# Two-layer backbone step: layer 1's seven products in another order with another plan of weights, and low parts of eight weights by an adding DMA

## The chip, the cores and the metric

The kernel runs on one core of a Trainium2 chip, as one launch. The metric is the device time of that core in microseconds (us), the median of several executions. A core has five engines with a queue of instructions each: TensorE (PE in the profile, with its weight loads as PEld), VectorE (DVE), ScalarE (ACT), GpSimd (POOL) and SyncE (SP), which here only issues DMAs. PSUM is the memory with eight banks into which PE writes, SBUF the memory that the engines compute from. The granted clock is the share of its full speed that TensorE is allowed; the profile gives it by slices.

## The reference

One inference step of a small network with two layers, on 640 tokens of width 1024: 512 latent tokens (`x_sample`) and 128 context tokens (`x_prompt`). Layer 0 mixes by attention and spatial gating, layer 1 by pooling over windows. Each layer ends in an MLP with a hidden width of 4096.

```python
def pool_mixer(h, w_pool, scale):          # layer 1: window means minus the token, times w_pool
...
def squared_relu_mlp(h, w1, w2):
    a = jax.nn.relu(h @ w1)
    return (a * a) @ w2
...
        x = x + g1 * mix
        h = rms_norm(x, norm2_g[l]) * (1 + sc2) + sh2
        x = x + g2 * squared_relu_mlp(h, w_ff1[l], w_ff2[l])
    return rms_norm(x, final_g), ckv_list, kpe_list
```

All of it is in fp32.

## The kernel before

**Numbers in two parts.** PE multiplies in a rounded fp32 format (fp32r). To stay near fp32 accuracy every operand is held as a high part, its rounded copy, and a low part, the rest. Each product is three matmuls, hi·hi, hi·lo and lo·hi, by `mm3` (L801 to L803). Activations lie with features on the partitions and tokens along the row, in two halves of 320 tokens (`C1`, index `ci`), so most matmuls are 128x128 weights by 320 columns.

**Weights.** A queue in program order, the class `Weights`, brings every weight from HBM. `loads` (L182) issues DMAs on SP into five raw buffers (`RAWB`). `pump` takes the next item of the queue, if its raw data are loading and a slot for the result is free: ACT copies it to the high part (L214), and a subtraction makes the low part (L216) on the engine that `st.lo` names, VectorE as a rule. A pump that finds no free slot does nothing. `need` pumps until a weight is there, `free` gives its slot back. In an MLP there are eight slots of 128x2x1024; where the program calls `pump` is thus a plan of when the splits stand in ACT's and DVE's queues.

**The passage between the layers.** In layer 0's last block `tick0` sets `st.lo = nc.gpsimd`, and the pooling stage follows: `pool_mm` does, for eight tiles of 128 features, two matmuls with `w_pool`, a residual on DVE, a square on ACT and an addition of the squares on DVE (L692 and L707), and pumps a weight at every second tile. The sum of squares goes through PE, whose `R_ps` matmuls (L718) spread it over the partitions, and `norm_h` makes layer 1's h in halves: ht on DVE (L744), its high part on ACT (L748), its low part on DVE (L752). Next to these, `turn1` steps through the string list `TURNS`: at each `w` it pumps a weight with `st.lo = nc.gpsimd`. So eight weights in all, `w1` of layer 1's blocks 0 and 1, have their low parts made by GpSimd (L216).

**Layer 1's MLP.** Its 4096 hidden features are eight blocks of four 128-row groups. Blocks 0 and 1 (`lead`) are computed in the plain way while h is still being made. For the blocks b = 2 to 7, `blocks7` calls `up7(b, p)` for p = 0 and 1. One call makes two groups, f = 2p and g = 2p+1, for both halves of the tokens, as a 2x2 product of blocks by seven multiplications in place of eight (the form of Strassen and Winograd). Its left factors are sums of w1's four quarters, made by `w1s_use` in place in two raw buffers that are kept for it: item i splits one quarter or sum into hi (L558) and lo (L559) and then prepares the next sum (L563). Each result is half a slot (`half`). Its right factors are quarters of h and the sums `B[0..3]`, made once by `sums`. `product(i, op, ps, first)` is 4 times three matmuls; with `first` false it adds into a bank that holds an earlier product. Four banks are used: pa, pd, pb and pc, out of a pool of six (`psm`). Before the change, p1 is the copy of product 0 (ACT, L1598), u2 = p1 + product 2, u3 = u2 + product 1 (DVE, L1581), and the outputs are, in this order,

- (g,1) = u3 + product 3
- (f,0) = product 0 + product 4, added up in bank pa
- (g,0) = u2 + (product 1 + product 5, in bank pd)
- (f,1) = u2 + (product 3 + product 6, in bank pc)

`finish` makes of an output r the squared relu and its two parts in `A`: Relu, Square and a copy on ACT (L1586 to L1588), and a subtraction on DVE (L1589), which `up7` places after the next output's addition. Behind the two calls, `down` multiplies by w2 (16 sums of 12 matmuls for a block; L1407 adds each to x on DVE). The first four, the early ones (`cut`), start on groups 0 and 1 alone, then groups 3 and 2 follow.

**Order.** Every engine takes its instructions in the program's order, so the position of a `st.pump()` or of a `lo()` in `up7` decides what stands ahead of what on ACT and DVE. A block of layer 1 has 18 items: 14 of `w1s`, of which those of p = 0 and 1 hold seven half slots each, and four of w2 with a slot each. In blocks 0 and 1 two of the eight slots are lent to `sums` (`spare`), which leaves six.

## Time and profile before

| | us |
|---|---|
| median of three runs | 1301.89 |
| lowest, highest | 1299.29, 1303.52 |
| the profiled execution's own time | 1302.88 |
| its span, first to last instruction | 1301.1 |
| TensorE busy in that span | 1261.8 (97%) |
| VectorE, ScalarE, GpSimd busy | 826.6, 549.3, 216.5 |
| mean granted clock | 0.989 |

The profile is one execution. Its slices are 1/40 of the span, 32.5 us each, and a digit is the busy share in tenths. A stretch in the table of windows gives its limits and length, then for each engine the busy time and the number of instructions, then the granted clock, the share of DMA and its rate. In the timeline a row is an instruction: start, duration, engine, line and tile, with the idle time before it and what ended it in brackets. The passage between the layers lies at 804 to 870 us, the blocks b = 2 to 7 behind 885.

### The profile page before, as it was taken

To read this page: it belongs to the slowest core of one execution; us is meant where nothing else is said; L and a number is where in the kernel's file an instruction comes from. 1 tells how busy PE (TensorE), PEld (TensorE's weight loads), DVE (VectorE), ACT (ScalarE), POOL (GpSimd) and SP (SyncE) were. 2 spreads that over 40 slices of the span, in tenths; PEclk is the share of its full clock that TensorE was granted. 3 is DMA by queue.
4 is the path that set the end of the run, shared out by engine and by line. 5 is a ranking of instruction groups with operands and counts; after the bars stand their busy time and mean duration, and the time that the engine had idled before them with its cause. 6 is when DMAs were issued, how large, how long until landed. Compare 5 with 4: busy or idle time off the path is not lost.

```text
span 1301.1 us, 20746 instructions
## 1 busy us (share of the span) xinstructions
PE 1261.8 (97%) x8308; PEld 1183.4 (91%) x8308; DVE 826.6 (64%) x1553; ACT 549.3 (42%) x993; POOL 216.5 (17%) x182
## 2 busy tenths in 40 slices
PE   7999999999999999999999999799999999999997
PEld 5899975689999999999999998789999999999997
DVE  5753864564766575666666638876887567675664
ACT  4445454453453434333343414534235435354353
POOL 0010312221113221313131315610000000000001
PEclk8999999999999999999999999899999999999999
DMA  7742286340335344444353431202113223132102
GB/s 291 261 164 72 81 227 234 131 170 25 116 117 160 113 145 131 150 126 157 119 161 114 147 130 33 97 1 79 52 35 112 80 67 98 38 111 84 61 33 82
DMA packets 63200, 149.89 MB, mean 115 GB/s; under 512 B 5072, under 2 KB 21968, under 8 KB 62592
## 3 DMA queue, kind: packets, MB, share of 16 engines
q1 hardware_dynamic: 61360, 142.53, 33.3%
q0 software_dynamic: 1456, 5.96, 1.9%
q8 instruction: 65, 1.06, 0.3%
q14 instruction: 31, 0.25, 0.1%
q10 hardware_dynamic: 288, 0.08, 0.0%
HBM read 140.02 MB, written 5.39 MB: 112 GB/s over the span
## 4 chain that ended last, share of the span: by engine, by line
PE 79%; DVE 10%; ACT 7%; issue 2%; DMA 1%; POOL 0%; DVEq 0%; ACTq 0%; POOLq 0%
PE dn_ps L802 11%; PE dn_ps L801 11%; PE dn_ps L803 11%; PE up_ps L801 7%; PE up_ps L803 7%; PE up_ps L802 7%; PE wo_ps L801 1%; PE o_ps L1302 1%; PE wo_ps L803 1%; PE wo_ps L802 1%; ACT r L1587 1%; DVE w L216 1%; ACT w L558 1%; ACT r L1586 1%; PE t_ps L1269 1%
## 5 line engine op out<-in xcount | busy, mean ns | idle before, releaser
L801 PE MATMUL dn_ps<-aa,w 128*128 128x320 f32 (+4 forms) x1024 | 319.1, 312 | 2.1 <-ACT aa L1588 2.1
L802 PE MATMUL dn_ps<-aa,w 128*128 128x320 f32 (+4 forms) x1024 | 318.4, 311 | 0.7
L803 PE MATMUL dn_ps<-aa,w 128*128 128x320 f32 (+4 forms) x1024 | 316.8, 309 | 0.0
L802 PE MATMUL up_ps<-h,w 128*128 128x320 f32 (+2 forms) x800 | 248.6, 311 | 6.0 <-DVE h L752 5.9
L801 PE MATMUL up_ps<-h,w 128*128 128x320 f32 (+2 forms) x800 | 249.6, 312 | 1.3 <-ACT h L748 1.3
L803 PE MATMUL up_ps<-h,w 128*128 128x320 f32 (+2 forms) x800 | 248.6, 311 | 0.0
L1407 DVE SCALAR_TENSOR_TENSOR x<-dn_ps,mod,x 128x320 f32<-128x320 f32 (+4 forms) x360 | 144.7, 434 | 115.0 <-PE dn_ps L803 113.2
L801 PEld LDWEIGHTS dn_ps<-aa,w 128*128 128x128 f32 x1024 | 193.1, 189 | 5.8 <-ACT aa L1588 4.1
L216 DVE TENSOR_TENSOR w<-raw,w 128x1024 fp32r<-128x1024 f32 (+4 forms) x122 | 151.3, 1250 | 70.9 <-ACT w L214 69.8
L802 PEld LDWEIGHTS dn_ps<-aa,w 128*128 128x128 f32 x1024 | 193.0, 188 | 2.5 <-DVE aa L1589 2.4
L803 PEld LDWEIGHTS dn_ps<-aa,w 128*128 128x128 f32 x1024 | 193.0, 189 | 0.0
L214 ACT ACTIVATE w<-raw 128x1024 fp32r<-128x1024 f32 (+4 forms) x131 | 132.0, 1026 | 112.0 <-DMA raw<-w_ff 85.0
L802 PEld LDWEIGHTS up_ps<-h,w 128*128 128x128 f32 x800 | 151.2, 189 | 8.1 <-DVE h L752 8.1
L801 PEld LDWEIGHTS up_ps<-h,w 128*128 128x128 f32 x800 | 151.0, 189 | 4.9 <-issue 3.4
L466 POOL TENSOR_TENSOR acc<-acc,raw 128x1024 f32<-128x1024 f32 x42 | 100.7, 2399 | 303.7 <-ACT raw L464 297.6
L803 PEld LDWEIGHTS up_ps<-h,w 128*128 128x128 f32 x800 | 151.0, 189 | 0.0
L559 DVE TENSOR_TENSOR w<-raw,w 128x512 fp32r<-128x512 f32 x84 | 57.7, 687 | 34.6 <-ACT w L558 33.7
L558 ACT ACTIVATE w<-raw 128x512 fp32r<-128x512 f32 x84 | 51.4, 624 | 61.9 <-DVE raw L563 57.1
L464 ACT ACTIVATE raw<-raw,cs 128x1024 f32<-128x1024 f32 x42 | 48.3, 1149 | 62.6 <-DVE acc L459 54.2
L1925 POOL TENSOR_TENSOR y<-y,fg 128x1024 f32<-128x1024 f32 x1 | 2.4, 2392 | 416.5 <-ACT y L1921 416.5
L1481 DVE TENSOR_TENSOR r<-r,up_ps 128x328 f32<-128x328 f32 (+2 forms) x80 | 37.6, 484 | 42.6 <-ACT r L1480 41.0
L1484 DVE TENSOR_TENSOR aa<-r,aa 128x640 fp32r<-128x640 f32 (+3 forms) x52 | 39.6, 762 | 35.6 <-ACT aa L1483 35.6
(404 smaller groups left out, 2122.1 us busy)
## 6 DMA issues: line engine op xcount, KB each, us to landing
raw<-w_ff SPq DMA_DIRECT2D x126, 512.0 KB, 3.6
raw<-w_mod SPq DMA_DIRECT2D x80, 512.0 KB, 3.9
raw<-w_m SPq DMA_DIRECT2D x16, 512.0 KB, 6.0
raw<-w_out SPq DMA_DIRECT2D x8, 512.0 KB, 4.4
kT<-ckvT POOLq DMA_DIRECT2D x4, 768.0 KB, 10.8
xr<-x SPq DMA_DIRECT2D x5, 512.0 KB, 5.5
xs<-x SPq DMA_DIRECT2D x2, 1280.0 KB, 9.3
x<-xs POOLq DMA_DIRECT2D x2, 1280.0 KB, 9.6
```

The lines of the kernel that those rows point to most:

```text
L214: self.nc.scalar.activation(out=w[:, 0, 0:size], in_=r, func=AF.Copy)
L216: lo.tensor_tensor(out=w[:, 1, 0:size], in0=r, in1=w[:, 0, 0:size].bitcast(F32), op=ALU.subtract)
L464: act(out=raw if k else acc[1], in_=raw, func=AF.Copy, scale=w[1])
L466: nc.gpsimd.tensor_tensor(out=acc[1], in0=acc[1], in1=raw, op=ALU.add)
L558: act(out=w[:, 0], in_=src, func=AF.Copy)
L559: vec.tensor_tensor(out=w[:, 1], in0=src, in1=w[:, 0].bitcast(F32), op=ALU.subtract)
L801: mm(ps, lhsT=st_[0], rhs=mv[0], start=first, stop=False, skip_group_check=on)
L802: mm(ps, lhsT=st_[0], rhs=mv[1], start=False, stop=False, skip_group_check=on)
L803: mm(ps, lhsT=st_[1], rhs=mv[0], start=False, stop=last, skip_group_check=on)
L1407: vec.scalar_tensor_tensor(out=xv, in0=ps[:, p0:p0 + c1 - c0], scalar=gate[:, d, m:m + 1], in1=xv, op0=ALU.mult, op1=ALU.add)
L1481: vec.tensor_tensor(out=rv, in0=rv, in1=ps, op=ALU.mult)
L1484: vec.tensor_tensor(out=aa[:, 1, lo:hi], in0=r[:, lo:hi], in1=aa[:, 0, lo:hi].bitcast(F32), op=ALU.subtract)
```

## The change

There are four parts.

1. `st.lo` is None in the pooling stage and at the `w` of `TURNS`. `pump` then has ACT write the low part's place with the high part times -1, and GpSimd issues a DMA that reads the weight from HBM once more and adds it to that place (512 KB each). The subtraction on GpSimd is gone.
2. `up7` takes the last three products in another order: product 4 goes into bank pd, for (g,0); product 5 into pc, for (f,1); product 6 into pa, for (f,0). `w1s_use` makes the sums in the order that this asks for. The second operation of `finish` for (f,0) is a multiplication on DVE in place of a Square on ACT, and the low part of (f,1) follows behind product 6.
3. The plan of weights: product i's half slot is given back one product later (the last at the end of `up7`). Of the pumps in `up7`, one behind product 1 is gone, and the others stand at other products. In the downs a pump stands behind every sum from the third on, and two follow at the end of the block.
4. The early downs take the second half of the tokens first (`C[::-1]`).

```diff
@@ Weights.pump
-                self.nc.scalar.activation(out=w[:, 0, 0:size], in_=r, func=AF.Copy)
-                lo = self.nc.gpsimd if key[0] in self.slow else self.lo
-                lo.tensor_tensor(
-                    out=w[:, 1, 0:size], in0=r, in1=w[:, 0, 0:size].bitcast(F32), op=ALU.subtract
-                )
+                hi, lo = w[:, 0, 0:size], w[:, 1, 0:size]
+                self.nc.scalar.activation(out=hi, in_=r, func=AF.Copy)
+                eng = self.nc.gpsimd if key[0] in self.slow else self.lo
+                if eng is None:
+                    self.nc.scalar.activation(out=lo, in_=hi.bitcast(F32), func=AF.Copy, scale=-1.0)
+                    src, shape = loads[0]
+                    if len(shape) == 2:
+                        lo = lo.rearrange("p (k n) -> p k n", k=shape[0])
+                    self.nc.gpsimd.dma_start(out=lo, in_=src, accum_op=ALU.add)
+                else:
+                    eng.tensor_tensor(out=lo, in0=r, in1=hi.bitcast(F32), op=ALU.subtract)
@@ w1s_use
-            src = (f0, g0, g0, f0, f1, g1, f1)[i]
+            src = (f0, g0, g0, f0, g1, g0, f1)[i]
...
-                    4: (f1, f1, g0, ALU.subtract)}.get(i)
+                    4: (g0, f1, g0, ALU.subtract)}.get(i)
@@ up7, product
-                st.free(("w1s", l, b, p, i))
+                gone.append(("w1s", l, b, p, i))
+                if i:
+                    st.free(gone.pop(0))
@@ up7, finish
-                act(out=r, in_=r if src is None else src, func=AF.Relu)
-                act(out=r, in_=r, func=AF.Square)
+                if src is not None:
+                    act(out=r, in_=src, func=AF.Relu)
+                    vec.tensor_tensor(out=r, in0=r, in1=src, op=ALU.mult)
+                else:
+                    act(out=r, in_=r, func=AF.Relu)
+                    act(out=r, in_=r, func=AF.Square)
@@ up7
             pd = product(1, 2, None, True)
-            st.pump()
             pb = product(2, 1, None, True)
...
             lo = finish(g, 1)
             st.pump()
-            pa = product(4, (0, 1), pa, False)
-            lo()
-            lo = finish(f, 0, pa)
-            if not p:
-                st.pump()
-            pd = product(5, 3, pd, False)
+            pd = product(4, 3, pd, False)
             add(out(g, 0), u2, pd)
             lo()
             lo = finish(g, 0)
-            pc = product(6, (1, 1), pc, False)
+            if not p:
+                st.pump()
+            pc = product(5, (1, 1), pc, False)
             add(out(f, 1), u2, pc)
             lo()
             lo = finish(f, 1)
-            lo()
             if not p:
                 st.pump()
+            pa = product(6, (0, 1), pa, False)
+            lo()
+            finish(f, 0, pa)()
+            st.free(gone.pop(0))
@@ blocks7
-                    early = cut(range(2), C) if b >= f0 else []
+                    early = cut(range(2), C[::-1]) if b >= f0 else []
...
-                        if j % 2 or j > 3:
+                        if j > 1:
                             st.pump()
                     free(1)
                     if b == f0 - 1:
                         bg.drain()
+                    st.pump(2)
                     continue
@@ tick0
-        st.lo = nc.gpsimd
+        st.lo = None
@@ turn1
-                st.lo = nc.gpsimd if t == "w" else vec
+                st.lo = None if t == "w" else vec
```

## The prediction

> **What bounds the kernel now.** I read the page first, then the busy time by stretches, then the timelines of GpSimd (POOL), VectorE (DVE) and ScalarE (ACT) in the two places that the change touches, then the chain of waits and the waits of TensorE (PE).

> ```profile
> span 1301.1 us, 20746 instructions
> PE 1261.8 (97%) x8308; PEld 1183.4 (91%) x8308; DVE 826.6 (64%) x1553; ACT 549.3 (42%) x993; POOL 216.5 (17%) x182
> PE   7999999999999999999999999799999999999997
> ```

> PE sets the time: 97% busy, and only slice 26 (813 to 846 us, the passage between the layers) drops inside the run. So an edit gains where PE waits, and loses where it makes PE wait. The stretches, with PE's, PEld's, DVE's, ACT's and POOL's busy time in that order, show how much there is:

> ```profile
> 804.00:814.00 10.00, 6.70 (x31) 5.01 (x29) 9.69 (x12) 6.00 (x10) 6.91 (x3) 1.00 0.35 105
> 814.00:822.00 8.00, 7.21 (x33) 7.21 (x33) 2.98 (x11) 1.13 (x3) 4.71 (x15) 0.57 0.43 131
> 822.00:844.00 22.00, 16.37 (x102) 14.32 (x101) 21.36 (x31) 14.77 (x29) 16.39 (x8) 1.00 0.28 96
> 844.00:870.00 26.00, 25.70 (x139) 22.95 (x139) 18.67 (x46) 9.56 (x22) 3.54 (x5) 0.93 0.00 1
> 885.00:960.00 75.00, 75.00 (x513) 75.00 (x512) 56.39 (x119) 25.43 (x47) 0.00 (x0) 1.00 0.21 68
> ```

> Between 804 and 844 PE is idle for 3.3 + 0.8 + 5.6 = 9.7 us of 40, DVE is full, and the granted clock falls to 0.57 for one stretch. From 885 to 960 PE has no gap: 75.00 us for 513 matmuls, 0.146 us each. That is the pace against which I measure the blocks later on.

> **The passage: what GpSimd costs there.** In the timelines (start, duration, then engine and line):

> ```profile
> 804.69 4.95 POOL L216 TENSOR_TENSOR w<-raw,w 128x1024 fp32r<-128x1024 f32 x2 [1.48 <-ACT w L214]
> 812.04 4.90 POOL L216 TENSOR_TENSOR w<-raw,w 128x1024 fp32r<-128x1024 f32 x2 [2.40 <-ACT w L214]
> 825.88 7.58 POOL L216 TENSOR_TENSOR w<-raw,w 128x1024 fp32r<-128x1024 f32 x3 [7.16 <-ACT w L214]
> 805.17 2.23 DVE L707 TENSOR_TENSOR sq<-sq 128x320 f32<-128x320 f32 x1
> 807.79 2.20 DVE L707 TENSOR_TENSOR sq<-sq 128x320 f32<-128x320 f32 x1
> 810.38 0.48 DVE L707 TENSOR_TENSOR sq<-sq 128x320 f32<-128x320 f32 x1
> 812.36 2.38 DVE L707 TENSOR_TENSOR sq<-sq 128x320 f32<-128x320 f32 x1 [0.18 <-ACT sq L692]
> 823.06 0.55 DVE L752 SCALAR_TENSOR_TENSOR h<-ht,mod,h 128x320 fp32r<-128x320 f32 x1 [0.23 <-ACT h L748]
> 826.02 2.61 DVE L752 SCALAR_TENSOR_TENSOR h<-ht,mod,h 128x320 fp32r<-128x320 f32 x1
> 803.57 1.04 ACT L214 ACTIVATE w<-raw 128x1024 fp32r<-128x1024 f32 x1
> 814.79 2.49 PE R_ps L718 x12
> 869.34 1.23 PE R_ps L718 x12
> 839.67 0.55 ACT L748 ACTIVATE h<-ht,mod 128x320 fp32r<-128x320 f32 x1
> 843.71 0.54 DVE L752 SCALAR_TENSOR_TENSOR h<-ht,mod,h 128x320 fp32r<-128x320 f32 x1
> ```

> The same DVE addition takes 0.48 us alone and 2.2 to 2.4 us when GpSimd is in one of its 2.45 us subtractions; the h of L752 goes from 0.55 to 2.61. The change takes all eight subtractions away (2 + 2 + 3 and one at 834). It adds for each weight a second ACT pass of 1.04 us, right behind the first in ACT's queue, and one DMA issue on GpSimd.

> First half. DVE loses 1.75 + 1.72 + 1.90 = 5.4 us of stretching. But the pooling stage's squares (0.40 us each in ACT's queue) stand behind those passes: from 803.57 ACT now has three weights at 2.02 and six squares at 0.40 ahead of the last addition, which ends at 803.57 + 6.06 + 2.40 + 0.3 = 812.3. The R_ps matmuls of 814.79 so start 2.5 us earlier, not 5.4. Second half, from the first ht (L744) at 821.8 to the last h at 843.71: DVE is freed of about 6.5 us, but ACT's work before the last L748 (13.1 us, from the first at 822.5 to 840.2 with its waits) grows by four passes to 17.1; it fills the same time, and DVE's last h, behind window sums that GpSimd still stretches, comes 0.8 us earlier by my queue count. Together 3.3 us.

> The clock. Its fall to 0.57 doubles the 12 R_ps pieces (2.49 against 1.23 at 869) and the twelve matmuls behind them: some 3 us. It followed 4.4 us with hardly a matmul. The idle time shrinks to about 2 us, and whether the clock then holds I take as even: 0 to 3.4 us, value 1.7. **Passage: 5 us gained, bounds 3.3 and 6.7.**

> ```profile
> PE up_ps L802 <- DVE h L752: 5.9, 7, 2.5
> ```

> The 0.93 after 844 followed a wait of this line, and none of its seven was longer than 2.5 us. [...]

> The DMAs. The trace shows no adding transfer. The nearest rows for 512 KB are:

> ```profile
> raw<-w_ff SPq DMA_DIRECT2D x126, 512.0 KB, 3.6
> kT<-ckvT POOLq DMA_DIRECT2D x4, 768.0 KB, 10.8
> x<-xs POOLq DMA_DIRECT2D x2, 1280.0 KB, 9.6
> ```

> So 3.6 to 10.8 us; adding reads the destination too, and I take 8, near the queue that GpSimd issues on. The first weight's two ACT passes end at 805.7; at 10.8 it lands by 817, and the first product that needs it starts at 817 to 820. The last one lands by 843 at 10.8, needed at about 843. Value 0. If this cover is gone, PE waits for the whole excess. Behind a waiting DMA issue in GpSimd's queue stand the sum of squares for the next norm and the window sums; both come later than the issue by that count. Raw buffers come free earlier, after ACT's first pass, and SP's loads (3.6 us each) with them: nothing waits for those.

> **The blocks: the products' order and the plan.** A block of layer 1 (six of them, b = 2 to 7) runs 14 products of 12 matmuls and 16 downs of 12: 360. The pieces of one, from the chain, the group table and the timelines:

> ```profile
> 1018.61 0.44 ACT p L1598
> 1072.61 0.44 ACT p L1598
> 1024.96 0.47 ACT L1586 ACTIVATE r<-r 128x320 f32<-128x320 f32 x1 [1.29 <-DVE r L1581]
> 1026.35 0.62 ACT L558 ACTIVATE w<-raw 128x512 fp32r<-128x512 f32 x1
> 1033.25 0.42 ACT L1598 ACTIVATE p<-up_ps 128x320 f32<-128x320 f32 x1
> 1027.00 0.69 DVE L559 TENSOR_TENSOR w<-raw,w 128x512 fp32r<-128x512 f32 x1 [2.07 <-ACT w L558]
> 1029.46 0.48 DVE L1581 TENSOR_TENSOR r<-u,up_ps 128x320 f32<-128x320 f32 x1
> 1037.43 0.49 DVE L1581 TENSOR_TENSOR u<-u,up_ps 128x320 f32<-128x320 f32 x1
> 1037.84 1.22 DVE L216 TENSOR_TENSOR w<-raw,w 128x1024 fp32r<-128x1024 f32 x1
> 1037.98 0.41 PE L801 MATMUL up_ps<-w 128*128 128x320 f32 x1
> 1045.54 0.41 PE L801 MATMUL dn_ps<-aa,w 128*128 128x320 f32 x1 [0.26 <-ACT aa L1588]
> L1481 DVE TENSOR_TENSOR r<-r,up_ps 128x328 f32<-128x328 f32 (+2 forms) x80 | 37.6, 484 | 42.6 <-ACT r L1480 41.0
> ```

> One block takes 1072.61 - 1018.61 = 54.0 us; 360 at 0.146 are 52.6. So 1.4 us a block is all that order can return. Its two waits are in the rows: at 1037.98 product 5 of p = 1 starts as u3 ends (1037.43 + 0.49), because it adds into pd's bank, which u3 reads; at 1045.54 the first down waits for the last halves of A.

> The new order takes the second wait away: the two last outputs are late by one operation fewer, C[1]'s downs go first, and the last half of A is needed 39 matmuls (5.7 us) after the last product against a chain of some 4. But pd is now added to by product 4, one product (1.75 us) sooner. Count from 1018.61. Product n of the 14 can start at 1.75 (n - 1) - 0.3: the twelfth (n = 11, product 4 of p = 1) at 17.2. When is u3 done? The finish of (g,1) starts at 6.35, as before (1024.96). Behind it, in program order, stand now for three outputs: three ACT operations (1.4), the hi of a weight (0.62), its lo on DVE (0.69, a wait on that hi), and only then the next output's addition on DVE (0.48), which starts ACT's next three. Before, the second of these, (f,0), came straight from PSUM, with no addition to wait for.

> - (g,1) 6.35; weight's hi 7.7 to 8.4; lo to 9.1; addition of (g,0) to 9.5
> - (g,0) to 10.9; hi to 11.5; lo to 12.2; addition of (f,1) to 12.7
> - (f,1) to 14.1; a w2's hi (1.04) to 15.1; Relu of (f,0) to 15.4; w2's lo (1.22) to 16.3; lo of (f,1), then the new product on DVE (0.48, the row of L1481) to 17.2; hi of (f,0) to 17.6
> - copy of p1 to 18.0 (before 1033.25 + 0.42, that is 15.1); next w2's hi to 18.9, lo to 20.1; u2, u3 to 21.1

> So product 4 of p = 1 waits 21.1 - 17.2 = 3.9 us, plus 0.1 for its slow first matmul. The block becomes 52.6 + 4.0 = 56.6, 2.6 us more. Are the pump's places filled? Layer 1 has eight slots less two lent to the sums. With each slot given back one product later, there is still one at each of the eight pumps by my count (items 0 and 1's after product 2, 2 and 3's after product 4, 4 and 5's after product 6), so yes. The later giving back costs nothing else, since no pump finds the slots full where one is needed. The two pumps moved to the block's end have room on DVE (35.9 busy of 54 in the whole block). The changed differences of weights cost the same operations.

> Six blocks: 6 x 2.6 = 15.7. I add 1 for b = 2, where the sums' backlog stands ahead, and 1 for the last block, whose first downs cover 18 matmuls, not 24 (both estimates from the count). **Blocks: 17.7 us lost**, bounds a gain of 1.4 x 6 = 8 and a loss of 24.

> **Sum.** -5 + 17.7 = +12.7 us. The profiled execution took 1302.9 (span 1301.1), 1 us above the median 1301.9; so 1315.6 there, and 1314 to 1315 in the median. I give 1314.

> **The rivals.** *The pump's places stay empty* (faster). If slots or raws are not there at p = 0's three pumps, the steps hi and lo of a weight vanish from the chain: 1.3 + 1.3 + 1.3 us, and u3 ends near 17.2. The point of decision is 3.9 us of chain; past it PE has no wait, each block gains 1.3, and the time is 1301.9 - 5 - 8 = 1289. For it: such a plan would be the sense of giving slots back late. Against it: my count finds a slot each time. Chance 0.18. *Halfway*, a wait of 1.5 to 2 us left: within 0.3%, 0.05. *The adding DMAs come late*: if each holds its queue for 6 us instead of the 4.6 that eight of them have between 806 and 843, PE waits 8 x 1.4 = 11 more: 1325. Against it: both bounds above are just covered. 0.08. *The passage doesn't get shorter*: ACT's second passes take the whole of DVE's gain, 1319 to 1320; ACT is free 7 of 22 us there, so 0.05. The forecast keeps 0.64, with its own range 1306 to 1322.

> **How the numbers follow.** Slower by over 0.3% (about what a measurement of this kernel can tell from no change): 0.64 + 0.08 + 0.05 = 0.77; within 0.05; faster 0.18. The range 1289 to 1325 holds the forecast, the halfway case, the short passage and half each of the first and third rivals.

> **What would show it.** In the profile after: DVE's L707 and L752 near 0.5 us in the passage and R_ps about 2.5 us earlier; ACT 8 us busier; in the blocks a period near 56.6, a wait of PE's up_ps on DVE's u of about 4 us in p = 1, and no wait of dn_ps on aa. I'm wrong if that wait is under 1 us, or if the waits of up_ps name a DMA.

## The result and the profile after

The changed kernel takes 1321.25 us (median of four runs, 1320.38 to 1323.49) against 1301.54 for the kernel before in the same comparison: a ratio of 1.0155, 95% interval 1.0134 to 1.0176. So it is 19.7 us slower. The forecast was 1314, slower, with a range of 1289 to 1325.

The page of the changed kernel, its span, busy times and the two rows of TensorE by slices:

```profile
span 1319.2 us, 20782 instructions
PE 1266.0 (96%) x8308; PEld 1193.5 (90%) x8308; DVE 823.2 (62%) x1565; ACT 551.4 (42%) x989; POOL 206.7 (16%) x182
PE   7999999999999999999999999899989898998987
PEclk8999899999999999999999998999989999999999
```

The number of matmuls is the same (8308), GpSimd has 10 us less to do, ScalarE 2.1 us more, and the dip of the passage (slice 26) is still there. New are the 8s from slice 30 on: holes in the blocks of layer 1. The waits of PE behind 880 us name them. The columns are: who waited for whom, us in total, times, the longest. First the kernel after, then the kernel before:

```profile
PE up_ps L808 <- DVE u L1593: 23.2, 7, 4.0
```

```profile
PE up_ps L801 <- DVE u L1581: 2.4, 2, 1.5
PE dn_ps L801 <- ACT aa L1588: 2.1, 7, 0.6
```

A wait for u, 3.5 us long in each of the blocks 3 to 7, stands where waits of half a us stood. In block 2 (it starts at 959.2 us before, at 954.4 after) product 4 waits in both calls, 4.3 us in p = 0 and 2.1 in p = 1, from the start of one matmul to the next. The wait of the downs (dn_ps) for the last halves of A has gone, as the change is made to do. Here is one of the new waits, at product 4 of p = 1 in one block, with the next block's, in PE's timeline:

```profile
1034.92 0.30 PE L810 MATMUL up_ps<-h,w 128*128 128x320 f32 x1
1038.71 0.51 PE L808 MATMUL up_ps<-w 128*128 128x320 f32 x1 [3.49 <-DVE u L1593]
1039.03 0.47 PE L809 MATMUL up_ps<-w 128*128 128x320 f32 x1
...
1096.78 0.56 PE L808 MATMUL up_ps<-w 128*128 128x320 f32 x1 [3.49 <-DVE u L1593]
```

From 1038.71 to 1096.78 is a block: 58.07 us, against 54.0 before. And the matmul behind the wait takes 0.47 where one takes 0.31 at full clock. What VectorE and ScalarE did meanwhile:

```profile
1032.59 1.23 DVE L225 TENSOR_TENSOR w<-raw,w 128x1024 fp32r<-128x1024 f32 x1 [2.09 <-ACT w L216]
1033.73 0.49 DVE L1606 TENSOR_TENSOR aa<-r,aa 128x320 fp32r<-128x320 f32 x1
1034.13 0.48 DVE L1601 TENSOR_TENSOR r<-r,up_ps 128x320 f32<-128x320 f32 x1
1036.42 1.23 DVE L225 TENSOR_TENSOR w<-raw,w 128x1024 fp32r<-128x1024 f32 x1 [0.78 <-ACT w L216]
1037.57 0.48 DVE L1593 TENSOR_TENSOR u<-p,up_ps 128x320 f32<-128x320 f32 x1
1038.08 0.49 DVE L1593 TENSOR_TENSOR u<-u,up_ps 128x320 f32<-128x320 f32 x1
```

```profile
1031.51 1.04 ACT L216 ACTIVATE w<-raw 128x1024 fp32r<-128x1024 f32 x1
1034.65 0.47 ACT L1605 ACTIVATE aa<-r 128x320 fp32r<-128x320 f32 x1 [1.77 <-DVE r L1601]
1035.03 0.42 ACT L1615 ACTIVATE p<-up_ps 128x320 f32<-128x320 f32 x1
```

Read it backwards from 1038.57, where u3 ends. It followed u2 (1037.57). U2 stood behind the low part of a w2 (1036.42), whose high part stood behind p1's copy (1035.03). The copy stood behind the last operation for (f,0) of p = 0 (1034.65), which ACT reached after 1.77 us of waiting for the product on DVE (1034.13), and that stood behind two low parts, of a w2 (1032.59) and of (f,1) (1033.73). This is the chain of the prediction, link by link.

Where the time went, at the same matmul of the program in both profiled executions (start in after less start in before):

```
up to 800 us, where the two programs are alike      -1.3
first matmul behind the twelve of R_ps              -4.9   (passage -3.6)
first matmul that needs the last h                  -4.8   (passage -3.5)
start of block 2                                    -4.8
start of blocks 3, 4, 5, 6, 7     -0.9, 3.1, 7.2, 11.3, 15.3
end                                                 18.1   (blocks +22.9)
```

The expectations of `passage_only` and `passage_vec` below put the second line at 3.2; the rows of R_ps (814.79 and 2.49 before, 810.85 and 1.50 after) give 3.6.

In the passage the additions on DVE are no longer stretched, and R_ps starts earlier. The additions in the groups of instructions between 799 and 850 us, first before, then after; then, all of after, a row each of ACT's timeline, of PE's and of the DMA issues:

```profile
L707 DVE TENSOR_TENSOR sq<-sq 128x320 f32<-128x320 f32 x6 | 8.3, 1375 | 0.2 <-ACT sq L692 0.2
```

```profile
L714 DVE TENSOR_TENSOR sq<-sq 128x320 f32<-128x320 f32 x6 | 2.9, 486 | 2.7 <-ACT sq L699 2.7
```

```profile
802.26 1.04 ACT L216 ACTIVATE w<-raw 128x1024 fp32r<-128x1024 f32 x1
```

```profile
810.85 1.50 PE L725 MATMUL R_ps<-ones,sq 128*128 128x1 f32 x12 [1.46 <-DVE sq L714]
```

```profile
w<-w_ff POOLq DMA_DIRECT2D x8, 512.0 KB, 10.0
```

An addition takes 0.49 us where it took 1.38 on average. The low parts of h (L752, after it L759) take 0.88 us on average where they took 1.48, not yet the 0.55 of one alone. The first weight's high part lies 1.31 us earlier than before (802.26 against 803.57), which is the lead from the beginning of the program. R_ps starts 3.94 us earlier, so 2.6 by the change, and its twelve pieces take 1.0 us less. DVE's additions now wait for ACT's squares (2.7 us), behind the second passes. An adding DMA lands 10.0 us after its issue.

### The profile page after: what moved, and what is told of

It reads as the page before. It is cut to its first block, busy times and chain, and to the rows that moved or that the text cites. A ratio compares the mean times of both kernels' runs of the same rounds, so it can differ in the third digit from the quotient of the medians.

```text
span 1319.2 us, 20782 instructions
## 1 busy us (share of the span) xinstructions
PE 1266.0 (96%) x8308; PEld 1193.5 (90%) x8308; DVE 823.2 (62%) x1565; ACT 551.4 (42%) x989; POOL 206.7 (16%) x182
## 4 chain that ended last, share of the span: by engine, by line
PE 75%; DVE 14%; ACT 7%; issue 2%; DMA 1%; POOL 0%; DVEq 0%; ACTq 0%; POOLq 0%
PE dn_ps L809 10%; PE dn_ps L808 10%; PE dn_ps L810 10%; PE up_ps L808 8%; PE up_ps L810 7%; PE up_ps L809 7%; ACT w L216 2%; DVE w L225 2%; DVE w L566 2%; DVE x L1414 2%; PE o_ps L1309 1%; PE wo_ps L808 1%; PE wo_ps L809 1%; PE wo_ps L810 1%; PE mod_ps L351 1%
## 5 line engine op out<-in xcount | busy, mean ns | idle before, releaser
L1414 DVE SCALAR_TENSOR_TENSOR x<-dn_ps,mod,x 128x328 f32<-128x328 f32 (+5 forms) x360 | 145.0, 434 | 114.5 <-PE dn_ps L810 113.6
L216 ACT ACTIVATE w<-raw 128x1024 fp32r<-128x1024 f32 (+4 forms) x131 | 132.7, 1026 | 114.1 <-DMA raw<-w_ff 86.9
L566 DVE TENSOR_TENSOR w<-raw,w 128x512 fp32r<-128x512 f32 x84 | 57.8, 688 | 40.2 <-ACT w L565 39.6
## 6 DMA issues: line engine op xcount, KB each, us to landing
raw<-w_ff SPq DMA_DIRECT2D x126, 512.0 KB, 3.7
raw<-w_mod SPq DMA_DIRECT2D x80, 512.0 KB, 3.9
raw<-w_m SPq DMA_DIRECT2D x16, 512.0 KB, 6.2
raw<-w_out SPq DMA_DIRECT2D x8, 512.0 KB, 4.3
w<-w_ff POOLq DMA_DIRECT2D x8, 512.0 KB, 10.0
kT<-ckvT POOLq DMA_DIRECT2D x4, 768.0 KB, 11.1
xr<-x SPq DMA_DIRECT2D x5, 512.0 KB, 5.6
xs<-x SPq DMA_DIRECT2D x2, 1280.0 KB, 8.9
```

The source lines that it names most:

```text
L216: self.nc.scalar.activation(out=hi, in_=r, func=AF.Copy)
L566: vec.tensor_tensor(out=w[:, 1], in0=src, in1=w[:, 0].bitcast(F32), op=ALU.subtract)
L1414: vec.scalar_tensor_tensor(out=xv, in0=ps[:, p0:p0 + c1 - c0], scalar=gate[:, d, m:m + 1], in1=xv, op0=ALU.mult, op1=ALU.add)
```

## The experiments

Below, the period of a block is the distance between the same matmul of successive blocks, b = 3 to 6. "Before" in a ratio is always the kernel before, run beside.

**The passage alone.** `passage_only` is the kernel before with part 1 of the change:

```diff
-        st.lo = nc.gpsimd
+        st.lo = None
...
-                st.lo = nc.gpsimd if t == "w" else vec
+                st.lo = None if t == "w" else vec
```

> The kernel before with part 1 of the change alone (low parts of the eight weights by ACT's second pass and an adding DMA). Theory: the passage gives 3.5 us by itself, nearly all of it before the R_ps matmuls (3.2 us earlier), and the blocks keep their period of 54.0; about 1298. Rival, that the passage's gain hangs on the blocks or is noise: 1301.5. Rival, that the DMAs cost something in the blocks: above 1301.5.

It took 1299.23 us, ratio 0.9983 (0.9970 to 0.9996). The passage ended 4.2 us earlier, of which 2.9 were left at the start of block 2; the period stayed at 54.0. So part 1 gains by itself, some 2 to 3 us, and doesn't touch the blocks.

**The order and the plan apart.** `old_order` keeps the new plan of weights and puts back the products, sums, finishes and early downs of before; `old_plan` keeps the new order and puts back the pumps and the giving back of slots. The core of the two, each against the changed kernel:

```diff
-            pd = product(4, 3, pd, False)
-            add(out(g, 0), u2, pd)
...
+            pa = product(4, (0, 1), pa, False)
+            lo()
+            lo = finish(f, 0, pa)
```

```diff
             pd = product(1, 2, None, True)
+            st.pump()
...
-                        if j > 1:
+                        if j % 2 or j > 3:
                             st.pump()
...
-                    st.pump(2)
```

> The changed kernel with the products, the sums of weights, the finishes and the early downs in the order of before, but with the new plan of weights (pumps, later giving back). Queue theory (the wait comes from order, plan and the product on DVE together, since all lengthen the chain ahead of u3 that product 4 waits for): period 54.3, no wait of 3.8 us, about 1299 to 1300. Rival, the plan alone makes the loss: period stays near 58.1, about 1321.

> The changed kernel with the pumps and the giving back of slots of before, but the new order. Queue theory: product 4 of p = 1 waits about 1.9 us for u3 and the same product of p = 0 about 0.5; below the length at which the clock falls, so period 55.4 and about 1308. Rival, the order alone with its early use of bank pd makes the loss: wait 3.8, period near 58, about 1320.

`old_order`: 1296.77 us, ratio 0.9946 (0.9927 to 0.9965), period 53.26. `old_plan`: 1329.70 us, ratio 1.0208 (1.0189 to 1.0227), periods 58.8 to 60.3. The first is better than expected, and the second goes the other way: the new plan is no part of the loss, in either order. With the order of before it gains 0.8 us a block (54.04 to 53.26), with the new order about 1.2. So the whole loss lies in what `old_order` puts back: the order of the products with the finish and the early downs that belong to it. DVE's timeline in `old_plan`, at the place shown above, tells why I had the sign wrong:

```profile
1157.83 2.36 DVE L225 TENSOR_TENSOR w<-raw,w 128x1024 fp32r<-128x1024 f32 x2 [0.78 <-ACT w L216]
1160.11 0.48 DVE L1590 TENSOR_TENSOR u<-p,up_ps 128x320 f32<-128x320 f32 x1
```

Two low parts of w2 stand ahead of u2, not one. In `old_order` there are two as well, yet PE does not stop. Its timelines of DVE and PE:

```profile
1027.03 2.50 DVE L225 TENSOR_TENSOR w<-raw,w 128x1024 fp32r<-128x1024 f32 x2 [0.46 <-ACT w L216]
1029.96 0.49 DVE L1593 TENSOR_TENSOR u<-u,up_ps 128x320 f32<-128x320 f32 x1
```

```profile
1029.30 0.31 PE L808 MATMUL up_ps<-h,w 128*128 128x320 f32 x1
...
1030.92 0.32 PE L810 MATMUL up_ps<-h,w 128*128 128x320 f32 x1
1031.07 0.31 PE L808 MATMUL up_ps<-w 128*128 128x320 f32 x1
```

While u3 is made, PE is in the product that adds into pa (1029.30 to 1031.07), a bank that nothing but p1's copy has to read. The order of before has this product first among the last three; the new order has it last.

**Which pump.** `pump_back` puts only the pump behind product 1 back into the changed kernel.

> The changed kernel with one pump put back: the one behind product 1 of each call of up7. If this pump is what the new plan gains (one splitting of w2 fewer ahead of u2 in p = 1): the wait of product 4 grows from 3.8 to 4.3 us, as with the whole old plan, period about 59. If the later giving back of slots or the pumps at the block's end are the plan's gain: wait 3.8 and period 58.1 as in the changed kernel.

1325.97 us in a single run, so without an interval; periods 58.7 to 59.9. The waits of a block came as 0.96 (p = 0) and 3.53 us (p = 1), not as one of 4.3; their sum is 4.5, against 3.8 in the changed kernel and 4.8 (0.53 and 4.29) with the whole old plan. All three are start to start, with the 0.15 us of a matmul in each. So this pump is about 0.7 of the plan's 1.0 us of waiting; the later giving back and the pumps at the end were not taken apart.

**The product on DVE.** `square_act` puts one operation of `finish` back:

```diff
-                if src is not None:
-                    act(out=r, in_=src, func=AF.Relu)
-                    vec.tensor_tensor(out=r, in0=r, in1=src, op=ALU.mult)
-                else:
-                    act(out=r, in_=r, func=AF.Relu)
-                    act(out=r, in_=r, func=AF.Square)
+                act(out=r, in_=r if src is None else src, func=AF.Relu)
+                act(out=r, in_=r, func=AF.Square)
```

> The changed kernel with one operation put back: the square of (f,0) on ACT in place of the product on DVE. Queue theory: the chain loses the way from ACT to DVE and back, during which DVE is held by a weight's low part; wait 2.6 us instead of 3.8, and if the clock falls only for the longer wait, no slow matmuls: period 55.6, about 1308. If the slow matmuls come with any wait: 57.0, about 1316. Rival, this operation is a trifle beside the bank: 1320 to 1321.

1310.83 us, ratio 1.0066 (1.0051 to 1.0081), between the two numbers expected. The wait is 2.6 us as expected, in every block from 3 on. Putting back this one operation, which the change brings along with the order, takes 10.4 us off (1321.25 to 1310.83). But the periods alternate: 56.87, 55.31, 56.87, 55.34. The granted clock behind four of these equal waits, in the table of windows (the clock is the number behind POOL's):

```profile
1036.00:1040.00 4.00, 4.00 (x17) 4.00 (x18) 1.51 (x3) 2.36 (x4) 0.00 (x0) 0.58 0.78 232
1093.00:1097.00 4.00, 4.00 (x29) 4.00 (x28) 1.51 (x3) 2.36 (x4) 0.00 (x0) 1.00 0.76 236
1148.00:1152.40 4.40, 4.26 (x20) 4.29 (x21) 1.91 (x3) 2.36 (x4) 0.00 (x0) 0.65 0.74 219
1205.00:1209.00 4.00, 3.98 (x27) 4.00 (x28) 1.50 (x3) 2.37 (x4) 0.00 (x0) 1.00 0.84 237
```

After two of them 17 and 20 matmuls went through (20 in 4.4 us) where 27 to 29 do at full clock. The fifth, in block 7, was not followed by slow matmuls either. So a wait of this length makes the clock fall or not, and my limit between 2.6 and 3.8 was no limit.

**The clock.** `warm` gives PE something to do in the wait; the sums are thrown away:

```diff
             pc = product(3, 0, None, True)
+            if p:
+                junk = psa.tile([128, 512], F32, tag="a", name="junk_ps")[:, 0:n]
+                h0 = H[0][0]
+                for i in range(18):
+                    mm(junk, lhsT=h0[:, 0, 0:128], rhs=h0[:, 0, 0:n], start=(i == 0), stop=(i == 17))
```

> The changed kernel with 18 matmuls (2.65 us) into an unused bank between product 3 and product 4 of p = 1; their sums are thrown away. The wait of product 4 stays as long in time, but PE is idle for only 1.2 us of it. If the granted clock falls because PE is idle: no slow matmuls behind the wait, period 58.1 - 1.5 = 56.6, about 1314. If the slow matmuls belong to product 4 itself (its operands, its bank): period 58.1, 1321.

1316.36 us, ratio 1.0115 (1.0088 to 1.0142), and the period is 56.57, as expected to 0.03. (The total is 2 us above the 1314 expected; 1.4 of them lie ahead of block 2, where this execution gained 2.0 in place of 3.5.) The same 3.5 us behind the wait, first in the changed kernel, then in `warm`:

```profile
1038.70:1042.20 3.50, 3.49 (x13) 3.50 (x14) 1.40 (x2) 2.00 (x4) 0.00 (x0) 0.52 0.78 216
```

```profile
1041.20:1044.70 3.50, 3.50 (x24) 3.50 (x25) 1.37 (x2) 2.04 (x4) 0.00 (x0) 1.00 0.77 214
```

13 matmuls against 24. The slow ones belong to PE's idleness, not to product 4. Useless matmuls make the kernel faster by 1.5 us a block from block 3 on; in block 2 the wait of 4.35 us is in p = 0, which they leave alone, and the clock falls there as before.

**The bank or the queue.** `own_bank` takes product 4's wait for u3 away by a bank of its own:

```diff
-            pd = product(4, 3, pd, False)
-            add(out(g, 0), u2, pd)
+            pe = product(4, 3, None, True)
+            add(out(g, 0), u3, pe)
```

> The changed kernel with a bank of its own for product 4, whose sum is then added to u3 (which holds product 1 already) in place of u2. Product 4 no longer waits for u3. Queue theory: ACT and DVE are as far behind as before, so the wait moves to product 5, which adds into the bank that the sum of (g,1), the next operation on DVE, reads; about 3.5 us there, period 57.8 to 58, 1319 to 1321. Bank theory: the wait goes for good, period 53 to 54, about 1298.

1321.51 us, ratio 1.0159 (1.0130 to 1.0189), period 57.87: no gain. The wait has moved to the next product, for r, which is the sum of (g,1):

```profile
PE up_ps L808 <- DVE r L1593: 22.7, 7, 3.9
```

So bank pd is only where the backlog of ACT and DVE is met. `w2_later` shortens the backlog itself: in p = 1 the pump behind p1 moves behind u3.

```diff
             act(out=p1, in_=pa, func=AF.Copy)
-            st.pump()
+            if not p:
+                st.pump()
...
             add(u3, u2, pd)
+            if p:
+                st.pump()
             st.pump()
```

> The changed kernel with the first pump of p = 1 moved from behind p1 to behind u3, so that one splitting of w2 (1.0 us on ACT, 1.2 on DVE) no longer stands ahead of u2. Queue theory: product 4 waits 1.2 to 1.9 us less, 1.9 to 2.6, and product 5 some 0.9 in addition; with the clock falling in half of the blocks at most, period 55.7 to 56.5, 1308 to 1313. If the way through ACT's finishes sets u3, not the splittings: 1320.

1308.08 us, ratio 1.0050 (1.0035 to 1.0065), period 55.47. Product 4 waits 1.8 us and product 5 1.0 (start to start), and the clock did not fall in any block from 3 on. The time is the lower end of what was expected, the period 0.2 us under it.

**A better version.** `old_order_ks` is `old_order` with another order of groups in two early downs:

```diff
-                        ps = down(b, d, c, ps, True, range(FB) if ps is None else (3, 2))
+                        ps = down(b, d, c, ps, True, range(FB) if ps is None else ((2, 3) if c is C[0] else (3, 2)))
```

> The order of before with the new plan and the passage by DMA, and one edit more: the early downs of the first half of the tokens end with group 2, then 3, in the order (2, 3), because the first output of p = 1's f is ready before that of g. The wait of the downs for the high part of (g,0), 0.35 to 0.4 us in each block, has three matmuls (0.44 us) more in front of it. If that wait is what is left: period 52.9 instead of 53.2, about 1295. If the group 2 parts are late as well: no change, 1297.

1293.47 us, ratio 0.9941 (0.9925 to 0.9957), period 52.83 in place of 53.26; a block's 360 matmuls at full pace are 52.7. So the blocks 3 to 6 have nothing left to give; block 2 still takes 57.7 us, 4.9 more, in waits of up to 1.7 us.

**The passage's other way, and its end.** `passage_vec` is the kernel before with the eight low parts subtracted on VectorE.

> The kernel before with the low parts of the eight weights of the passage by subtraction on VectorE, in place of GpSimd, and no adding DMA. If GpSimd's stretching of VectorE's operations is the passage's loss, VectorE gets 1.22 us for each weight and loses the 1.7 to 1.9 us of stretching: R_ps about 1.2 us earlier (against 3.2 by the DMA), the second half within a us of before; 1300. If VectorE's own work is the bound all through the passage, it is no better than before: 1301 to 1304.

1304.81 us, ratio 1.0026 (1.0013 to 1.0039); R_ps 1.3 us later, the passage's end 2.1 later. My count of 1.2 us earlier fell: by the second of the two theories VectorE's own work bounds the passage, and GpSimd, for all its stretching, took more from it than it cost. The adding DMA is better than either since it takes the work from both.

But after the change PE still waits 3.7 us for the last h. The changed kernel's row of that wait, its timeline of DVE, and ACT's row for that h:

```profile
PE up_ps L809 <- DVE h L759: 4.6, 3, 3.7
```

```profile
834.95 0.85 DVE L1867 TENSOR_TENSOR win<-hh 128x668 f32<-128x668 f32 x1
835.83 1.84 DVE L1867 TENSOR_TENSOR win<-win 128x664 f32<-128x664 f32 x1
837.60 1.85 DVE L759 SCALAR_TENSOR_TENSOR h<-ht,mod,h 128x320 fp32r<-128x320 f32 x1
```

```profile
834.14 0.55 ACT L755 ACTIVATE h<-ht,mod 128x320 fp32r<-128x320 f32 x1
```

The high part is there at 834.69; the low part starts 2.9 us later, behind two window sums. Two runs moved it, on top of `old_order_ks`: `last_h_first` with `'w0011'` for `'w0101'` in TURNS, `last_h_early` with `'11W101'` for `'11W11'`.

> old_order_ks with one edit in the passage: the last low part of h goes ahead of a step of window sums that stood before it in VectorE's queue (a string of TURNS is w0011 in place of w0101). In the trace after, the last h starts 2.9 us after its high part is ready, and PE waits 3.7 us for it. If this order on VectorE, not the low parts of the weights, sets the passage's end since the change: PE's wait falls under 1 us, 3 to 3.8 us gained, about 1290. If the window sums are then late for the pooling products: less than 1 us gained, 1293.

> old_order_ks with one step of TURNS moved, so that the last low part of h stands ahead of two window sums (0.85 and 1.84 us) in VectorE's queue and behind three short ones. (In last_h_first the marks that were exchanged stood behind that operation already, so the order in question was not changed.) If this order sets the passage's end since the change: PE's longest wait for h goes from 3.7 us to about 1.1, without a fall of the clock behind it; 2.6 to 4 us gained, about 1289. If another operation for h or the clock takes its place: under 1 us gained, 1292 to 1293.

`last_h_first` did not change the order in question (the window sums come from earlier strings) and is a second `old_order_ks`: 1291.69 us, ratio 0.9927 (0.9900 to 0.9953). `last_h_early`: **1288.80 us, ratio 0.9905 (0.9888 to 0.9922)**, the fastest version of the study. Its passage ends 7.2 us earlier than in before, not 3.9 as in `old_order_ks`; 5.2 are left at the start of block 2. PE's waits from the passage on, first rows:

```profile
PE up_ps L808 <- DVE u L1593: 2.4, 2, 1.3
PE up_ps L810 <- DMA w<-w_ff: 1.6, 2, 1.2
PE R_ps L725 <- DVE sq L714: 1.5, 1, 1.5
```

The long wait for h has gone from the list, and a wait for an adding DMA (1.6 us) has come: with h earlier, the 10.0 us that such a transfer took in the changed kernel are no longer covered.

## Why the prediction was right, and where its sizes were wrong

**The place and the cause: right.** Product 4 of p = 1 waits for u3, in each block from 3 on, 3.6 us (1038.71 less 1034.92, less one matmul of 0.15) for the 3.9 of the count. `old_order` showed that the order with its finish makes the loss, `own_bank` that the bank is not the cause but the backlog, `square_act` and `w2_later` that the wait shrinks when a link is taken out of the chain (by 1.2 and 2.0 us).

**The term that was mis-sized: "plus 0.1 for its slow first matmul".** The period was forecast as 52.6 + 4.0 = 56.6 and is 58.1. The difference is the clock: some 12 matmuls at 0.267 us (start to start) in place of 0.147 behind each wait, 1.45 us. `warm`, where the clock holds from block 3 on, has 56.57. With 18 slow matmuls in block 2 that is 5 x 1.45 + 2.1 = 9.3 us in all. I had seen the clock fall in the passage of the kernel before (0.57 from 814 to 822 us, behind 4.4 us with hardly a matmul), priced it there, and did not ask whether a wait of 3.9 us that I was forecasting myself would do the same.

**The ends of the blocks: too dear.** Without the clock, block 2 lost 1.8 us and the last one 1.4, where I had 3.6 for each; the two estimates of 1 us had the wrong sign. So the blocks lost 22.9 us for 17.7: 9.3 of the clock were not in the sum, 4.0 at these ends were too much in it, and by luck the second error hid part of the first. (6 x 2.6 is 15.6, not 15.7; nothing hangs on it.)

**The passage: the queue count right, the clock wrong.** R_ps started 2.6 us earlier for 2.5, and the passage gained 3.5 us for 3.3 by the count of the queues. The 1.7 us that I added for a clock that might hold did not come; from 804 to 844 us the granted clock is lower than before (after, then before):

```profile
804.00:844.00 40.00, 33.18 (x180) 30.98 (x179) 28.65 (x57) 29.24 (x53) 18.30 (x25) 0.83 0.92 211
```

```profile
804.00:844.00 40.00, 30.28 (x164) 26.54 (x162) 34.03 (x52) 21.89 (x42) 28.01 (x25) 0.91 0.33 105
```

DVE was not full all through the passage before, as the prediction's text has it: its row for 814 to 822 us shows 2.98 us of 8. The DMAs were hidden, as forecast, at 10.0 us and not 8; `last_h_early` shows how near the end of that cover is.

**The plan of weights: its sign.** I let it cost nothing. It gains, in both orders; in the new order mostly because one pump fewer stands ahead of u2 (`pump_back`), in the order of before its parts were not taken apart.

**Two signs that did not come.** ScalarE is 2.1 us busier, not 8: the second passes cost it 8.5 us, but the twelve squares that the change moves to VectorE (0.47 us each), which the forecast of this sign left out, take 5.6 off. And the low parts of h came down to 0.88 us, not to 0.5.

Together, in the profiled executions: -1.3 (a lead from the part where both programs are alike) - 3.5 + 22.9 = 18.1 us, for -5 + 17.7 = 12.7. The rivals fell: the pumps found their places, the wait was not halved, no DMA was waited for, and the passage did get shorter.

## What to carry to other kernels

Count the queues of the engines beside the bound one from the moment at which the bound one must read their result: a reordering that takes a wait from the end of a stage can put the backlog before an operation that has no slack, and the wait then grows by all that stands in those queues. Put first among the last products the one that needs nothing from them. And a forecast wait of TensorE needs a price for the clock behind it: here 1.45 us behind a wait of 3.6, and behind one of 2.6 the same or nothing, by where it fell.

## What the runs showed of the hardware that was not expected

Of PE's waits in the blocks 2 to 7, over all profiles of this study and measured start to start, all 27 of 3.5 us and more were followed by slow matmuls (9 to 21 of them), two of the seven between 2.5 and 3.1 us were, and none of those up to 2.1 us. A wait of 1.56 us at 865 to 875 us, the same in all fourteen profiles, was followed by 13 or 14 slow matmuls in six of them and by none in the others (by none in before, where it ends at 874.03, and in after, at 869.22); that alone moves an execution by 1.5 us, and is a good part of why the passage's gain at the start of block 2 lies anywhere from 2.0 to 3.5 us among kernels that are alike up to there.

```profile
1033.26:1036.67 3.41, 1.15 (x8) 0.92 (x8) 2.98 (x4) 1.31 (x2) 0.00 (x0) 1.00 0.71 185
1091.29:1094.70 3.41, 1.88 (x13) 1.91 (x14) 2.89 (x5) 0.61 (x2) 0.00 (x0) 1.00 0.72 235
1145.90:1149.31 3.41, 1.17 (x8) 1.20 (x9) 3.38 (x5) 0.86 (x1) 0.00 (x0) 1.00 0.68 204
1203.93:1207.34 3.41, 2.32 (x16) 2.35 (x17) 2.44 (x5) 0.87 (x2) 0.00 (x0) 1.00 0.72 211
1258.54:1261.95 3.41, 1.59 (x11) 1.62 (x12) 3.17 (x5) 0.61 (x2) 0.00 (x0) 1.00 0.00 0
```

Behind the first and the third, with PE busy for 1.15 and 1.17 us, the clock is 0.50 for the next stretch; behind the others, with 1.59 us and more, it stays at 1.00. The same holds of all waits over 1.2 us in the blocks 2 to 7 of these profiles: where 2.2 us or more of one stretch passed without a matmul (one counted as 0.15 us), the clock fell at its edge, and where it was 1.8 us or less it did not. In the changed kernel, the wait from 961.30 to 965.65 has 2.3 us in the stretch that ends with the fall at 963.72, and the one from 980.13 to 982.18 has at most 1.4 in one, with no fall. The fourteen waits of 1.56 us divide in the same way, but lower: six lay with 1.36 us or more in one stretch and were followed by a fall, eight with 1.23 or less (0.92 in before, 1.08 in after) and were not. This is read from the records; no run moved a wait against the edges on purpose, and none shows why the two limits differ.

In the passage the fall can also come late. In the changed kernel R_ps starts at 810.85 after 1.8 us without a matmul (row above), and the twelve matmuls behind it begin at full clock:

```profile
813.15 0.31 PE L808 MATMUL dn_ps<-aa,w 128*128 128x312 f32 x1
813.29 0.30 PE L809 MATMUL dn_ps<-aa,w 128*128 128x312 f32 x1
813.44 0.38 PE L810 MATMUL dn_ps<-aa,w 128*128 128x312 f32 x1
813.61 0.47 PE L808 MATMUL dn_ps<-aa,w 128*128 128x312 f32 x1
```

The clock goes from 1.00 to 0.50 at 813.53, in the middle of dense matmuls. Of the 3.41 us before it, from 810.12, 0.7 passed before R_ps began, and some 1.4 went to twelve matmuls of a single column each. PE's busy time in this stretch is 2.69 us, more than in any of the five above, so PE's busy time, as the profile counts it, does not part the falls from the rest here. What does, no run shows.
